# The weight sums of a 20-product down projection: from POOL to DVE

## Chip, cores and metric

The kernel runs on one core of one Trainium2 chip. The metric is the device time of one execution, in microseconds (us), as a median of several runs. Lower is better.

## What is computed

The reference is one step of a small streaming encoder with two layers, on 1024 prompt frames and 128 sample frames (8 streams of 16), 1152 tokens of width 1024 in all, float32 throughout:

```python
for layer in range(DEPTH):                       # DEPTH = 2: layer 0 is mixer A, layer 1 is mixer B
    ...                                          # norm, projections, chunked attention, output projection
    hp = hp + mlp(hp, g_mlp[layer], w_up[layer], w_down[layer])
    hs = hs + mlp(hs, g_mlp[layer], w_up[layer], w_down[layer])

def mlp(x, g_norm, w_up, w_down):
    return jnp.square(jax.nn.relu(rmsnorm(x, g_norm) @ w_up)) @ w_down
```

`w_up` is 1024 x 4096, `w_down` is 4096 x 1024. The change touches the last product of `mlp`, the down projection.

## The kernel before

Each layer runs through attention (with its projections), `wo_phase`, `mlp_up` and `mlp_down`. A float32 matmul is done in three passes: an operand is split into a high part, which ScalarE (ACT) rounds off in a cast (L128), and a low part, which VectorE (DVE) forms by subtracting the high part (L134, in `split`). Then `mm3` (L744) adds high x high, high x low and low x high into one bank of PSUM. These are the lines L746, L747 and L748 of the profile.

**The down projection** (`mlp_down`, L971) multiplies the block matrices by a scheme with 20 products instead of the usual number. It runs it twice in a layer, once for each half of the 4096 inner columns, so a layer has 40 products in a list `seq`. One product n takes:

- `a`: a combination of blocks of the activations, formed already in `mlp_up` (`forms_even`, `forms_odd`; the sums of tiles h and ht, L923 to L968) and stored by POOL's queue to DRAM (`hd`, L911). It is loaded by SP (`load_h`) and split in place: ACT casts, DVE subtracts (a<-a).
- `w`: one block of `w_down`, or a sum or difference of two. The raw blocks `r` (128 x 2048 elements, 1 MB) are loaded by SP (`load_w`). Where the product needs two of them, `add_w` (L1051) forms the sum in a buffer `s` (two of them, in turn); this is L1067. The last four products of a layer write it over a raw block instead. `split_w` (L1069) then splits w and a.
- 36 matmuls: three banks of 128 tokens each x 4 blocks of the inner dimension x 3 passes.
- additions: the three banks are added to or subtracted from tiles `x` of the residual (L1119), for none, one or two of the six output blocks.

The tables `W_FORMS`, `OUT_FORMS` and `CHAINS` at the top of the file say which blocks a product reads and which outputs it is added to. By these tables a layer has 32 products with two raw blocks and 8 with one; 8 products that add nothing, 23 that add one set of three banks, 9 that add two sets. Products of one chain go on accumulating in the same three banks, so within a chain the next product's first matmul on a bank waits for the L1119 that reads this bank. There are six banks in turn (`c=(6, 1)`), two buffers w and three a.

**Order.** A planner orders the instructions of each engine ahead of time: it simulates the program in time and gives each engine, among the instructions that are ready, the one that stands first in the program. Each engine then runs its queue strictly in that order and waits on semaphores. In the program the loop over n issues the loads for product n + 3, the splits for n + 1, the sum for n + 2, the matmuls and additions of n, and then the loads of further a. SP issues its loads in one fixed chain (`load`, L1030).

Of the kernel before, what the change touches and what calls it, by code (L numbers as in the profile page):

```python
# [11 lines left out]
ALU = mybir.AluOpType  # L12
# [82 lines left out]
class Build:  # L95
# [875 lines left out]
    def mlp_down(self, layer, out):  # L971
        nc = self.nc
        tt = nc.vector.tensor_tensor
        wd = self.ins["w_down"][layer].rearrange("(c g h p) n -> g h p c n", g=2, h=2, p=P)
        with ExitStack() as st:
# [11 lines left out]
            def take(tag):  # L987
                return slots.pop(tag) if tag in slots else fresh(tag)
# [60 lines left out]
            src = {}  # L1049

            def add_w(n):  # L1051
                if n >= total:
                    return
                s, p, g, *_, raws = seq[n]
                used = [(r, f) for r, f in enumerate(W_FORMS[p]) if f != "."]
                g = g if p not in NEG_H[s] else 1
                x, y = (raws[used[i][0]] for i in (0, -1))
                if len(used) == 1:
                    assert g == 1
                    src[n] = x  # L1060
                    return
                src[n] = x if n >= total - TAIL + 2 else take(f"s{n % 2}")
                plus = used[1][1] == "+"
                assert g == 1 or not plus
                if g < 0:
                    x, y = y, x
                nc.gpsimd.tensor_tensor(src[n], x, y, ALU.add if plus else ALU.subtract)  # L1067

            def split_w(n):  # L1069
                if n >= total:  # L1070
# [15 lines left out]
            for n in range(AHEAD):  # L1086
# [3 lines left out]
                if n in X_AT:  # L1090
                    load_x(X_AT[n])
            add_w(0)
            split_w(0)
            add_w(1)
            for n, (s, p, g, first, final, reads, _) in enumerate(seq):
                if layer == 0 and n == RANK:
# [3 lines left out]
                if n + AHEAD in X_AT:  # L1100
                    load_x(X_AT[n + AHEAD])
                split_w(n + 1)
                add_w(n + 2)
                if first:
                    banks = [self.psum("c", [P, 512], "ps_c") for _ in range(3)]
                a, w = aa.pop(n), ws.pop(n)
                for i in range(3):
# [9 lines left out]
                    for o, v in reads:  # L1117
                        x = xs[PARTS[o // 2][i]][:, N[o % 2]]
# [717 lines left out]
```

## Time and profile before

| | before |
|---|---|
| median of 3 runs | 2477.91 us (2471.18 to 2479.93) |
| the profiled execution, its own time | 2474.45 us |
| span from its first to its last instruction | 2472.3 us |
| granted TensorE clock, mean | 0.980 |
| first layer's down stage, about | 803 to 1198 us |
| second layer's down stage, about | 2079 to 2468 us |
| sums (L1067) | 64 on POOL |

In the profile PE is the matmul engine and PEld its weight loads, DVE is VectorE, ACT is ScalarE, POOL is GpSimd and SP the queue that issues most DMAs. A row of a group reads: line, engine, operation, what it writes <- what it reads, shape, count | busy us, mean ns of one | idle us of the engine just before, and what ended it. Matmuls overlap one another, so the spacing of their starts says more than their durations.

### The profile page before, as it was taken

The numbers are of one execution on the slowest core, as the hardware profiler recorded it, in microseconds if no ns is written. First come the engines' busy times: TensorE is split into PE (matmuls) and PEld (weight loads), VectorE is DVE, ScalarE is ACT, GpSimd is POOL, SyncE is SP. The second block draws the span as 40 slices with busy tenths as digits, with TensorE's granted clock in tenths as the row PEclk, the third lists the DMA queues.
The fourth block names the chain that finished last, engine by engine and source line by source line (L and its number), as shares of the span: only waits on it lengthen the run. The fifth ranks groups of instructions, "written<-read, shape, count | busy, mean of one in ns | idle before, by whom it ended". The sixth has DMA issues, their size and how long they took to land.

```text
span 2472.3 us, 33316 instructions
## 1 busy us (share of the span) xinstructions
PE 2311.3 (93%) x11429; PEld 1911.4 (77%) x11429; DVE 1848.3 (75%) x3128; ACT 1273.0 (51%) x2503; POOL 914.6 (37%) x956
## 2 busy tenths in 40 slices
PE   8998999999999789989999999998999998899989
PEld 6787877888888667767778788786888887677767
DVE  6788787665665888999577867877656566798995
ACT  3777674655555333333277766655555554233332
POOL 4434334122322554553233434344222223444650
PEclk9999999999999999999999999998999999899999
DMA  7445554243434643525544655543334336524523
GB/s 249 126 116 162 167 175 166 92 146 116 163 131 178 250 150 105 197 79 195 167 144 133 189 163 169 181 157 129 125 119 149 131 130 225 187 94 141 175 74 130
DMA packets 216376, 375.38 MB, mean 152 GB/s; under 512 B 51144, under 2 KB 125840, under 8 KB 216208
## 3 DMA queue, kind: packets, MB, share of 16 engines
q1 hardware_dynamic: 193136, 300.89, 37.8%
q0 software_dynamic: 21776, 67.65, 7.5%
q10 hardware_dynamic: 1296, 4.72, 0.5%
q8 instruction: 90, 1.47, 0.3%
q14 instruction: 78, 0.64, 0.1%
HBM read 241.23 MB, written 130.90 MB: 151 GB/s over the span
## 4 chain that ended last, share of the span: by engine, by line
PE 62%; DVE 18%; DMA 9%; issue 6%; ACT 3%; POOL 1%; SPq 0%; DVEq 0%; ACTq 0%; POOLq 0%
DVE a L134 5%; PE ps_x L746 5%; PE ps_x L748 5%; PE ps_x L747 5%; DVE w L134 3%; DMA a<-hd 3%; DVE x L1119 3%; PE ps_mm L217 3%; PE ps_c L746 3%; PE ps_c L747 3%; PE ps_c L748 3%; PE ps_mm L219 3%; PE ps_mm L218 3%; PE ps_y L748 2%; PE ps_y L747 2%
## 5 line engine op out<-in xcount | busy, mean ns | idle before, releaser
L746 PE MATMUL ps_c<-w,a 128*128 128x512 f32 x960 | 386.3, 402 | 62.2 <-DVE x L1119 54.7
L747 PE MATMUL ps_c<-w,a 128*128 128x512 f32 x960 | 385.0, 401 | 24.0 <-DVE w L134 23.9
L1067 POOL TENSOR_TENSOR s<-r,r 128x2048 f32<-128x2048 f32 x56 | 291.2, 5202 | 281.2 <-DVE w L134 160.4
L748 PE MATMUL ps_c<-w,a 128*128 128x512 f32 x960 | 383.1, 399 | 5.4 <-DVE a L134 5.4
L911 POOL DMA_DIRECT2D hd<-h x272 | 147.9, 544 | 582.4 <-ACT h L820 280.0
L134 DVE TENSOR_TENSOR a<-a 128x1536 fp32r<-128x1536 f32 x80 | 258.5, 3232 | 46.4 <-ACT a L128 46.4
L746 PEld LDWEIGHTS ps_c<-w,a 128*128 128x128 f32 x960 | 185.9, 194 | 113.7 <-DVE x L1119 36.9
L747 PEld LDWEIGHTS ps_c<-w,a 128*128 128x128 f32 x960 | 185.9, 194 | 67.6 <-DVE w L134 29.4
L128 ACT CAST a<-a 128x1536 fp32r<-128x1536 f32 x80 | 118.5, 1481 | 213.9 <-DMA a<-hd 213.8
L748 PEld LDWEIGHTS ps_c<-w,a 128*128 128x128 f32 x960 | 186.0, 194 | 47.1 <-DVE a L134 8.0
L128 ACT CAST w<-s 128x2048 fp32r<-128x2048 f32 x56 | 107.1, 1912 | 212.0 <-PE ps_c L748 177.9
L134 DVE TENSOR_TENSOR w<-s,w 128x2048 fp32r<-128x2048 f32 x56 | 176.3, 3150 | 21.8 <-ACT w L128 21.7
L1119 DVE TENSOR_TENSOR x<-x,ps_c 128x512 f32<-128x512 f32 x246 | 158.8, 676 | 35.7 <-PE ps_c L748 35.5
L217 PE MATMUL ps_mm<-w,hh 128*128 128x512 f32 x432 | 172.9, 401 | 6.5 <-POOL w L185 2.1
L219 PE MATMUL ps_mm<-w,hl 128*128 128x512 f32 x432 | 171.9, 399 | 1.2 <-DMA hl<-hTd 1.0
L218 PE MATMUL ps_mm<-w,hh 128*128 128x512 f32 x432 | 170.9, 396 | 1.4 <-DVE w L190 1.1
L746 PE MATMUL ps_x<-sx,w 128*128 128x512 f32 (+1 forms) x408 | 158.9, 390 | 3.4 <-ACT h L867 2.5
L747 PE MATMUL ps_x<-sx,w 128*128 128x512 f32 (+1 forms) x408 | 155.2, 380 | 0.0
L748 PE MATMUL ps_x<-sx,w 128*128 128x512 f32 (+1 forms) x408 | 155.2, 380 | 0.0
L128 ACT CAST w<-ru 128x512 fp32r<-128x512 f32 (+1 forms) x160 | 110.0, 708 | 84.4 <-PE ps_y L747 32.0
L134 DVE TENSOR_TENSOR ptl<-ps_tr,pth 128x512 fp32r<-128x512 f32 x180 | 122.4, 685 | 23.5 <-ACT pth L128 18.0
L134 DVE TENSOR_TENSOR w<-ru,w 128x512 fp32r<-128x512 f32 (+1 forms) x160 | 126.6, 793 | 15.2 <-ACT w L128 15.1
(280 smaller groups left out, 5972.6 us busy)
## 6 DMA issues: line engine op xcount, KB each, us to landing
a<-hd SPq DMA_DIRECT2D x80, 768.0 KB, 4.2
hd<-h POOLq DMA_DIRECT2D x272, 192.0 KB, 2.5
ru<-in_w_up SPq DMA_DIRECT2D x64, 512.0 KB, 3.8
r<-in_w_down SPq DMA_DIRECT2D x32, 1024.0 KB, 8.7
x<-xd SPq DMA_DIRECT2D x41, 512.0 KB, 6.4
o<-oTd SPq DMA_DIRECT2D x52, 256.0 KB, 4.4
xd<-xo SPq DMA_DIRECT2D x18, 512.0 KB, 2.8
xo<-xd SPq DMA_DIRECT2D x18, 512.0 KB, 3.7
```

What stands on the lines that cost most here:

```text
L128: a = nc.scalar.copy(hi, src)
L134: return a, e.tensor_tensor(lo, src, hi.bitcast(F32), ALU.subtract)
L217: nc.tensor.matmul(ps, a, w[:, 0, k, :], start=(k == 0), stop=False)
L218: nc.tensor.matmul(ps, a, w[:, 1, k, :], start=False, stop=False)
L219: self.lp = nc.tensor.matmul(ps, b, w[:, 0, k, :], start=False, stop=(k == KC - 1))
L746: a = mm(ps, ah, bh, start=first, stop=False, skip_group_check=True)
L747: mm(ps, ah, bl, start=False, stop=False, skip_group_check=True)
L748: return a, mm(ps, al, bh, start=False, stop=last, skip_group_check=True)
L911: return lambda p, z: self.nc.gpsimd.dma_start(self.hd[c // 4][:, p, c % 4], z)
L1067: nc.gpsimd.tensor_tensor(src[n], x, y, ALU.add if plus else ALU.subtract)
L1119: tt(x, x, banks[i], ALU.add if v > 0 else ALU.subtract)
```

## The change

The sums and differences of two weight blocks are formed by VectorE instead of GpSimd. `tt` is `nc.vector.tensor_tensor`, set at the top of `mlp_down`. Operands, shapes and the place in the program stay.

```diff
@@ add_w, in mlp_down @@
                 if g < 0:
                     x, y = y, x
-                nc.gpsimd.tensor_tensor(src[n], x, y, ALU.add if plus else ALU.subtract)
+                tt(src[n], x, y, ALU.add if plus else ALU.subtract)
```

## Prediction, made before the change was run

> **What bounds the kernel now.** I read the page first (busy shares, costliest groups), then the two down stages by windows, then the rows of the sums, and last the engines' rows in order of time.
>
> ```profile
> span 2472.3 us, 33316 instructions
> ...
> PE 2311.3 (93%) x11429; PEld 1911.4 (77%) x11429; DVE 1848.3 (75%) x3128; ACT 1273.0 (51%) x2503; POOL 914.6 (37%) x956
> ...
> L746 PE MATMUL ps_c<-w,a 128*128 128x512 f32 x960 | 386.3, 402 | 62.2 <-DVE x L1119 54.7
> L747 PE MATMUL ps_c<-w,a 128*128 128x512 f32 x960 | 385.0, 401 | 24.0 <-DVE w L134 23.9
> L1067 POOL TENSOR_TENSOR s<-r,r 128x2048 f32<-128x2048 f32 x56 | 291.2, 5202 | 281.2 <-DVE w L134 160.4
> ```
> ```profile
> L134 DVE TENSOR_TENSOR a<-a 128x1536 fp32r<-128x1536 f32 x80 | 258.5, 3232 | 46.4 <-ACT a L128 46.4
> L134 DVE TENSOR_TENSOR w<-s,w 128x2048 fp32r<-128x2048 f32 x56 | 176.3, 3150 | 21.8 <-ACT w L128 21.7
> ...
> L134 DVE TENSOR_TENSOR w<-r,w 128x2048 fp32r<-128x2048 f32 x24 | 68.4, 2849 | 18.3 <-ACT w L128 18.3
> ```
>
> Over the span PE looks like the bound, but where it idles in the down stage it waits for DVE: 54.7 us for L1119 (a product's banks added into x) and 23.9 us for L134 (the low half of w). The sums of the change (L1067) are POOL's, and POOL idles 281.2 us ahead of them, most of it until DVE has released a buffer s. So POOL is not the bound of the stage by its own work. The next view says how much of the stage is not matmul. It is cut into products 0 to 5, 6 to 35 and 36 to 39 of each layer (36 matmuls a product: 216, 1080, 144).
>
> ```profile
> 803.60:871.80 68.20, 53.86 (x216) 41.98 (x215) 11.84 (x18) 0.92 0.72 253
> 871.80:1157.30 285.50, 254.62 (x1080) 205.08 (x1081) 62.84 (x98) 0.98 0.40 134
> 1157.30:1197.20 39.90, 35.62 (x145) 27.66 (x143) 4.08 (x6) 0.96 0.52 181
> 2079.10:2151.10 72.00, 56.06 (x216) 44.34 (x216) 11.80 (x18) 0.86 0.58 210
> 2151.10:2433.10 282.00, 257.28 (x1081) 207.52 (x1081) 62.72 (x98) 0.96 0.36 122
> 2433.10:2468.00 34.90, 33.40 (x145) 26.69 (x143) 4.17 (x7) 1.00 0.38 127
> ```
>
> (Columns: the stretch, its length, busy time of PE, PEld and DVE on this tile, granted clock, DMA share, GB/s.) An undisturbed product takes 8.16 us: three matmuls start 0.68 us apart (the first two PE rows below), and a product has twelve such threes. So the six stretches would take 49.0, 244.8, 32.6, 49.0, 244.8 and 32.6 us; they are longer by 19.2, 40.7, 7.3, 23.0, 37.2 and 2.3 us. Together 129.7 us is all that these stages can give. Why the 30 middle products take 9.5 us each is seen in the rows by time:
>
> ```profile
> 2194.99 2.28 DVE L134 TENSOR_TENSOR w<-s,w 128x2048 fp32r<-128x2048 f32 x1
> 2197.19 0.67 DVE L1119 TENSOR_TENSOR x<-x,ps_c 128x512 f32<-128x512 f32 x1
> 2197.79 5.79 DVE L134 TENSOR_TENSOR a<-a 128x1536 fp32r<-128x1536 f32 x1
> 2203.50 1.27 DVE L1119 TENSOR_TENSOR x<-x,ps_c 128x512 f32<-128x512 f32 x2
> 2204.70 2.27 DVE L134 TENSOR_TENSOR w<-s,w 128x2048 fp32r<-128x2048 f32 x1
> 2206.90 1.74 DVE L134 TENSOR_TENSOR a<-a 128x1536 fp32r<-128x1536 f32 x1
> ```
> ```profile
> 2197.34 4.62 POOL L1067 TENSOR_TENSOR s<-r,r 128x2048 f32<-128x2048 f32 x1 [5.09 <-DVE w L134]
> 2207.05 6.07 POOL L1067 TENSOR_TENSOR s<-r,r 128x2048 f32<-128x2048 f32 x1 [5.09 <-DVE w L134]
> ```
> ```profile
> 2201.90 0.39 PE L748 MATMUL ps_c<-w,a 128*128 128x512 f32 x1
> ...
> 2202.58 0.39 PE L748 MATMUL ps_c<-w,a 128*128 128x512 f32 x1
> 2204.23 0.50 PE L746 MATMUL ps_c<-w,a 128*128 128x512 f32 x1 [1.26 <-DVE x L1119]
> ```
>
> (Columns: start, duration, engine, instruction.) The same a<-a subtraction takes 5.79 us when a POOL sum began shortly before it, and 1.74 us when it began first; then the sum takes 6.07 instead of 4.62 us. The first sum ends at 2201.96 and a<-a at 2203.58, that is 1.62 us later: it did nothing until POOL had finished. The two engines exclude each other here, and whichever starts second waits. DVE is thereby busy without a break: w, x, a, x, x, and again w 9.71 us after the last (2194.99 to 2204.70), while PE waits 1.26 us for an x addition that stands behind a<-a. DVE's lost time sets the pace.
>
> **The change, part by part.** The rows for the prices:
>
> ```profile
>   DMA r<-in_w_down: 116.7, 15
> ```
> ```profile
> L134 DVE TENSOR_TENSOR a<-a x80: 1739/1759/6099, 795.5 to 2457.4; 128x1536 fp32r<-128x1536 f32 x80
> ```
>
> (The first row: how long POOL sat idle ahead of L1067 until r had landed, and how often. The second: minimum, median and maximum of a<-a in ns.) Added on DVE: 64 sums, 56 into s by the row above and 8 in place by the code (the last four of a layer). DVE has no plain sum of this shape in the trace; the nearest row is w<-s,w, the same two SBUF operands of 2048 elements, at 2.28 us where nothing holds it (2194.99 above). From below it could not be under a<-a's 1.74 us (1536 elements), from above 3.15 us, the mean of w<-s,w with its waits. I take 2.28, since the waits were for POOL: 64 x 2.28 = 146 us.
>
> Removed from DVE: the waits inside its own instructions. a<-a falls from 3.23 to 1.76 us, 80 x 1.47 = 118 us; w<-s,w from 3.15 to 2.28 us, 56 x 0.87 = 49 us. The 24 w split straight from r fall from 2.85 to 2.28 us, 14 us. In the first products two small sums of the stage before are held too:
>
> ```profile
> L943 DVE TENSOR_TENSOR ht<-h 128x384 f32<-128x384 f32 x1 | 5.0, 4974 | 0.0
> L939 DVE TENSOR_TENSOR ht<-h 128x384 f32<-128x384 f32 x1 | 4.9, 4879 | 0.0
> ...
> L935 DVE TENSOR_TENSOR h<-h 128x384 f32<-128x384 f32 x1 | 0.5, 547 | 0.0
> ```
>
> Those two (groups of the stretch from 780 to 860 us) lose 4.4 and 4.3 us against the 0.55 of the third. I take it that the second layer has such a pair as well: 17 us. In all 118 + 49 + 14 + 17 = 198 us leave and 146 come: DVE is relieved by about 52 us while it takes over all the sums. POOL is empty in these stages afterwards but for the stores of h. At the start of a stage these queue behind the sums; they come out earlier at no cost. The sums' sources are loaded as before by SP, whose queue holds the loads of a and x too; nothing is moved on it. Outside the two stages the instructions are the same; the planner may place some of them otherwise, which I set at nothing, since no row says which way.
>
> What is on the path: the middle products. A product with one bank set to add costs DVE 2.28 (w) + 1.74 (a) + 2.28 (sum) + 1.94 (three x: 0.67 and 1.27) = 8.24 us, and consecutive instructions overlap by a little (the 9.71 us cycle holds 10.01 us of them), so about 7.9 us against PE's 8.16. PE takes over as the bound, narrowly. The scheme's tables give 23 such products of 40 in a layer; 8 add nothing (6.0 us) and 9 add two bank sets (9.7 us). Eight products need no sum (2.28 us less). Following both through the order, only five stretches of a product ask DVE for 9.7 us: 5 x 1.5 = 8 us, and 2 us for order: 10 us left of 40.7, 10 of 37.2. The sum is off PE's path as long as w waits for the release of its buffer, not for s: ACT's cast of w starts when PE ends the product two before, and then that cast and the 2.28 us of w fill only half of a product.
>
> Start: PE waits there for loads and for x, of which the held pair explains 8.7 us less the two new sums, 4.6 us. I take 5 us off each: 14 and 18 left. End: no sum stands in those products; the 7.3 and 2.3 us stay. Left over: 14 + 10 + 7 + 18 + 10 + 2 = 61 of 129.7, so 69 us are saved. The profiled execution took 2474.45 us (span 2472.3), so it would take 2405; the median of the three runs, 2477.91, lies 3.5 us above it, and against the median that is 2409 us.
>
> Part of this comes through the clock, so it hangs on long idle times going away:
>
> ```profile
> 2174.54 0.79 PE L746 MATMUL ps_c<-w,a 128*128 128x512 f32 x1 [3.69 <-DVE x L1119]
> ...
> 2179.82 0.42 PE L746 MATMUL ps_c<-w,a 128*128 128x512 f32 x1
> ```
>
> After an idle time of 3.69 us the next twelve matmuls take 5.28 us (from row to row, eleven lie between) instead of 12 x 0.227 = 2.72: a tail of 2.6 us beyond the gap itself.
>
> **The rivals.** *Slower: sums that block DVE.* DVE runs its queue in order. POOL waited 116.7 us, 15 times, for r to arrive, with little else behind it. If the planner puts a sum into DVE's queue ahead of its landing, the splits and the x additions behind it wait as well, and PE after them. For it: 7.8 us a wait is more than the 4 us or so by which w is early. Against it: several of these waits lie at the start, where PE waits for loads of the same queue, and a sum two products ahead can be planned late. It decides from 69 / 15 = 4.6 us of each wait that reaches PE. With 5.5 us of each and ten slow-clock tails: 2409 + 83 + 26 = 2518 us.
>
> *Slower: a saturated DVE.* The middle stretches have DVE busy nearly throughout; if its busy time were work, 32 x 2.28 = 73 us a stage would lengthen both:
>
> ```profile
> 803.00:1198.00 395.00, 345.50 (x1453) 276.31 (x1452) 341.85 (x239) 136.53 (x89) 183.99 (x60) 0.97 0.47 160
> 2079.00:2468.00 389.00, 346.86 (x1442) 278.63 (x1440) 335.94 (x217) 132.63 (x82) 173.69 (x46) 0.95 0.40 139
> ```
>
> DVE (third figure) would stand at 415 and 409 us in stages of 395 and 389: 20 us longer each, 2478 + 40 = 2518 us. The 1.74 beside 5.79 us speaks against it. The Trainium skill, Perfetto Trace Analysis, section "Optimizing Scalar/DVE Operations", advises moving work off a saturated DVE, to GPSIMD even, which is the other way from this change; it adds that the two share an SBUF read port so that such a move might not help, and the trace agrees with this second half (a<-a held to 5.79 us behind a sum).
>
> *No change.* A sum on DVE comes just before an x addition for which PE waits. If half of the 64 do, 32 x 2.28 = 73 us come back: 2409 + 73 = 2482 us. The rows leave room for a sum behind w, where PE has just got its bank, so I hold it unlikely.
>
> **How the numbers follow.** Forecast 0.74; blocked sums 0.13, saturated DVE 0.05, no change 0.08. The forecast's own range is 2380 (all 78 us of the middle and 20 of the starts saved) to 2440 (half of the middle kept). Within 0.5%, about what a measurement of this kernel can tell from no change, means 2465.5 to 2490.3 us. The no-change case reaches out of it at both ends, 0.02 of it to the faster side. Faster 0.76, same 0.06, slower 0.18. For 8 in 10 the range goes to 2495, which leaves out the larger part of the slower cases, and begins at 2380.
>
> **What would show it.** Right: L1067 on DVE at about 2.3 us; a<-a at a mean near 1.8 and w<-s,w near 2.3 us; PE's idle time for L1119 well under 54.7 us; the middle stretches near 255 us, at a clock of 0.99 or 1.00; DVE's busy time some 50 us lower. Wrong: DVE idle before L1067 for r<-in_w_down with PE waiting behind it (first rival); L1067 or a<-a above 3 us with POOL empty, which would refute the exclusion; PE's waits for L1119 as long as before while a<-a is short (no change).

## The result and the profile after

With the sums on DVE the kernel takes 2402.07 us (median of 4 runs, 2399.86 to 2404.34). The kernel before, beside it, took 2474.55 us. The ratio is 0.9708, with a 95% interval of 0.968 to 0.9736: about 72 us less. The profiled execution has a span of 2399.8 us, 72.5 us less than before.

The page of the kernel after (busy shares, then the groups that answer to those shown of before; columns as there):

```profile
PE 2291.6 (95%) x11429; PEld 1903.1 (79%) x11429; DVE 1787.2 (74%) x3192; ACT 1272.6 (53%) x2503; POOL 573.2 (24%) x892
...
L746 PE MATMUL ps_c<-w,a 128*128 128x512 f32 x960 | 380.3, 396 | 29.7 <-ACT a L128 15.9
L747 PE MATMUL ps_c<-w,a 128*128 128x512 f32 x960 | 378.9, 395 | 5.2 <-DVE w L134 5.2
...
L134 DVE TENSOR_TENSOR a<-a 128x1536 fp32r<-128x1536 f32 x80 | 140.4, 1755 | 56.0 <-ACT a L128 56.0
...
L134 DVE TENSOR_TENSOR w<-s,w 128x2048 fp32r<-128x2048 f32 x56 | 127.9, 2284 | 15.5 <-ACT w L128 15.5
...
L1067 DVE TENSOR_TENSOR s<-r,r 128x2048 f32<-128x2048 f32 x56 | 127.7, 2284 | 2.8 <-DMA r<-in_w_down 2.8
```

DVE has 64 instructions more and is 61 us less busy, because a<-a went from 3232 to 1755 ns and w<-s,w from 3150 to 2284 ns. PE's idle time before L746 fell from 62.2 to 29.7 us, and the largest part of it is no longer DVE's x addition (54.7 us before, 13.7 now) but ACT, which waits for a load of a. The wait for w at L747 fell from 23.9 to 5.2 us.

The down stages of the kernel after, cut into products 0 to 5, 6 to 35 and 36 to 39 of each layer (stretch, length, busy PE, PEld and DVE on the banks, granted clock, DMA share, GB/s):

```profile
805.30:871.30 66.00, 54.93 (x217) 43.72 (x217) 11.82 (x18) 0.90 0.68 245
871.30:1127.20 255.90, 247.57 (x1081) 201.85 (x1080) 63.90 (x98) 1.00 0.46 153
1127.20:1167.60 40.40, 36.86 (x145) 28.46 (x143) 4.13 (x7) 0.92 0.53 181
2045.10:2110.10 65.00, 53.84 (x216) 42.64 (x216) 11.81 (x18) 0.92 0.64 234
2110.10:2360.80 250.70, 246.47 (x1082) 202.16 (x1081) 63.84 (x98) 1.00 0.41 138
2360.80:2395.50 34.70, 33.32 (x145) 26.64 (x143) 4.26 (x8) 1.00 0.39 128
```

The two middle stretches lost 29.6 and 31.3 us (285.5 and 282.0 before), the starts 2.2 and 7.0, the ends nothing. Sum of the six: 782.5 us before, 712.7 after, so 69.8 of the 72.5 us lie where the sums are. The clock in the middle is 1.00, where it was 0.98 and 0.96.

The steady cycle, DVE's rows by time in the kernel after (start, duration):

```profile
944.93 2.29 DVE L134 TENSOR_TENSOR w<-s,w 128x2048 fp32r<-128x2048 f32 x1 [0.16 <-ACT w L128]
947.14 0.68 DVE L1119 TENSOR_TENSOR x<-x,ps_c 128x512 f32<-128x512 f32 x1
947.74 2.28 DVE L1067 TENSOR_TENSOR s<-r,r 128x2048 f32<-128x2048 f32 x1
949.94 1.75 DVE L134 TENSOR_TENSOR a<-a 128x1536 fp32r<-128x1536 f32 x1
951.61 1.28 DVE L1119 TENSOR_TENSOR x<-x,ps_c 128x512 f32<-128x512 f32 x2
953.13 2.29 DVE L134 TENSOR_TENSOR w<-s,w 128x2048 fp32r<-128x2048 f32 x1 [0.25 <-ACT w L128]
```

Five pieces of work, w to w in 8.20 us, and 0.16 to 0.25 us of slack ahead of each w: DVE now waits, by way of ACT's cast, for PE. Before, the same cycle without the sum took 9.71 us.

### The profile page after: what moved, and what is told of

Read it like the earlier page. It is cut to its first block, busy times and chain, and to the rows that moved or that the text cites. A ratio compares the mean times of both kernels' runs of the same rounds, so it can differ in the third digit from the quotient of the medians.

```text
span 2399.8 us, 33255 instructions
## 1 busy us (share of the span) xinstructions
PE 2291.6 (95%) x11429; PEld 1903.1 (79%) x11429; DVE 1787.2 (74%) x3192; ACT 1272.6 (53%) x2503; POOL 573.2 (24%) x892
## 4 chain that ended last, share of the span: by engine, by line
PE 68%; DVE 14%; DMA 8%; issue 4%; ACT 3%; POOL 1%; SPq 1%; ACTq 0%; DVEq 0%; POOLq 0%
PE ps_x L746 5%; PE ps_x L748 5%; PE ps_x L747 5%; PE ps_c L748 5%; PE ps_c L746 5%; PE ps_c L747 5%; PE ps_mm L219 4%; PE ps_mm L217 4%; PE ps_mm L218 4%; PE ps_y L748 2%; PE ps_y L747 2%; PE ps_y L746 2%; DVE w L134 2%; PE ps_tr L324 2%; DVE x L1119 2%
## 5 line engine op out<-in xcount | busy, mean ns | idle before, releaser
L746 PE MATMUL ps_c<-w,a 128*128 128x512 f32 x960 | 380.3, 396 | 29.7 <-ACT a L128 15.9
L747 PE MATMUL ps_c<-w,a 128*128 128x512 f32 x960 | 378.9, 395 | 5.2 <-DVE w L134 5.2
L748 PE MATMUL ps_c<-w,a 128*128 128x512 f32 x960 | 378.8, 395 | 4.7 <-DVE a L134 4.5
L128 ACT CAST a<-a 128x1536 fp32r<-128x1536 f32 x80 | 118.6, 1482 | 242.5 <-DMA a<-hd 240.1
L746 PEld LDWEIGHTS ps_c<-w,a 128*128 128x128 f32 x960 | 183.0, 191 | 75.5 <-ACT a L128 18.0
L748 PEld LDWEIGHTS ps_c<-w,a 128*128 128x128 f32 x960 | 182.8, 190 | 46.9 <-DVE a L134 8.5
L747 PEld LDWEIGHTS ps_c<-w,a 128*128 128x128 f32 x960 | 182.9, 191 | 44.0 <-DVE w L134 6.6
L134 DVE TENSOR_TENSOR a<-a 128x1536 fp32r<-128x1536 f32 x80 | 140.4, 1755 | 56.0 <-ACT a L128 56.0
L128 ACT CAST w<-s 128x2048 fp32r<-128x2048 f32 x56 | 107.2, 1914 | 126.7 <-PE ps_c L748 119.0
L746 PE MATMUL ps_x<-sx,w 128*128 128x512 f32 (+1 forms) x408 | 158.4, 388 | 3.7 <-ACT h L867 2.7
L747 PE MATMUL ps_x<-sx,w 128*128 128x512 f32 (+1 forms) x408 | 154.8, 379 | 0.0
L128 ACT CAST w<-ru 128x512 fp32r<-128x512 f32 (+1 forms) x160 | 110.0, 708 | 84.4 <-PE ps_y L747 32.0
L134 DVE TENSOR_TENSOR w<-s,w 128x2048 fp32r<-128x2048 f32 x56 | 127.9, 2284 | 15.5 <-ACT w L128 15.5
L1067 DVE TENSOR_TENSOR s<-r,r 128x2048 f32<-128x2048 f32 x56 | 127.7, 2284 | 2.8 <-DMA r<-in_w_down 2.8
```

Of the source, the lines that this page charges most:

```text
L128: a = nc.scalar.copy(hi, src)
L134: return a, e.tensor_tensor(lo, src, hi.bitcast(F32), ALU.subtract)
L746: a = mm(ps, ah, bh, start=first, stop=False, skip_group_check=True)
L747: mm(ps, ah, bl, start=False, stop=False, skip_group_check=True)
L748: return a, mm(ps, al, bh, start=False, stop=last, skip_group_check=True)
L1067: tt(src[n], x, y, ALU.add if plus else ALU.subtract)
```

## Experiments

The theory to be tested is the prediction's: POOL's sums and DVE's instructions with two operands in SBUF shut each other out, and the time that DVE stood still set PE's pace. Rivals: the sums are simply ready sooner on DVE (2.28 us instead of 4.6 or more; ACT waited 34.1 us for POOL's sums); or the planner rearranged the program. On the last, the traces of the two kernels have the same order of instructions on PE and on ACT throughout both down stages, and DVE's differs by a few places beside the inserted sums.

**POOL kept busy, with work that nobody needs.** Behind each sum on DVE, POOL reads one column of s (so that it starts at that point) and then works on a scratch tile in place (`gap`, which the kernel before holds but doesn't use). These kernels differ in the kind and the number of POOL's instructions only. The first, with two operands (the line that names `gap` is left out):

```diff
+            tt_junk = self.gap[:, 0:512]
+            nc.gpsimd.memset(tt_junk, 0.0)
...
+                nc.gpsimd.tensor_copy(tt_junk[:, 0:1], src[n][:, 0, 0:1])
+                for _ in range(4):
+                    nc.gpsimd.tensor_tensor(tt_junk, tt_junk, tt_junk, ALU.subtract)
```

> The changed kernel, and behind each of the 64 sums on DVE four idle POOL subtractions of 128x512 (about 1.28 us each by L700 to L703, 5.1 us together), on a scratch tile that nobody reads. Exclusion theory (DVE and POOL instructions with two SBUF operands shut each other out): per product with a sum 5.1 us of POOL and 6.3 us of DVE (w, a, sum) can't overlap, 11.4 us against PE's 8.16, so a<-a and w<-s,w above 2.3 and 2.8 us in the mean and a time of 2480 to 2610 us. Lateness theory (the gain came from sums that are ready sooner than POOL's were): a<-a stays at 1.76 us and the time at 2395 to 2412 us.

Measured: 2468.07 us, ratio to before 0.9973 (0.9959 to 0.9986). Its groups of the scratch work and of DVE:

```profile
L1073 POOL TENSOR_TENSOR gap<-gap 128x512 f32<-128x512 f32 x256 | 521.9, 2039 | 19.6
L134 DVE TENSOR_TENSOR a<-a 128x1536 fp32r<-128x1536 f32 x80 | 173.3, 2166 | 39.9 <-ACT a L128 39.9
L134 DVE TENSOR_TENSOR w<-s,w 128x2048 fp32r<-128x2048 f32 x56 | 146.9, 2624 | 7.5 <-ACT w L128 7.5
```

The sums stand where they do in the kernel after, and 66 of the 72 us are gone; by windows, some 51 us of this lie in the middle stretches (280.8 and 277.2 us). By itself this doesn't settle the lateness: the sums are held too. ACT's casts of w, the first to need a sum, waited for them as follows, before, after and here (behind the bar: idle time, and what ended it):

```profile
L128 ACT CAST w<-s 128x2048 fp32r<-128x2048 f32 x56 | 107.1, 1912 | 212.0 <-PE ps_c L748 177.9 <-POOL s L1067 34.1
L128 ACT CAST w<-s 128x2048 fp32r<-128x2048 f32 x56 | 107.2, 1914 | 126.7 <-PE ps_c L748 119.0 <-DVE s L1067 5.2 <-DVE a L134 2.6
L128 ACT CAST w<-s 128x2048 fp32r<-128x2048 f32 x56 | 107.0, 1911 | 184.8 <-PE ps_c L748 155.0 <-DVE s L1070 24.3 <-DVE x L1125 5.5
```

The kernel with the sums in pieces, below, decides that. Here the time is 12 us below the expected range, a<-a at 2.17, not above 2.3 us, and w<-s,w at 2.62, not above 2.8: DVE is held less than a sum of both engines' work would have it, and POOL more (a subtraction that takes 1.04 us at the least takes 2.04 in the mean). What DVE loses here is 33 us in a<-a (80 x 0.41), 19 us in w<-s,w and some 29 us in the other w and the sums.

**No operand read.** The same with eight memsets in place of the loop's four subtractions.

```diff
-                for _ in range(4):
-                    nc.gpsimd.tensor_tensor(tt_junk, tt_junk, tt_junk, ALU.subtract)
+                for _ in range(8):
+                    nc.gpsimd.memset(tt_junk, 0.0)
```

> As pool_two, but eight POOL memsets of 128x512 (no operand read, only written; about 0.5 us each from L583's 0.21 us for 128x128). The Trainium skill, SBUF — State Buffer, section "SBUF: two separate sides", says that a DVE instruction with two SBUF inputs is shut out only by a GpSimd one that reads SBUF. By that rule a<-a stays at 1.76 us and the time at 2395 to 2412 us. If writing alone shuts out as well, a<-a above 2.1 us and 2440 to 2560 us. This kernel also shows whether the added small read of s by POOL costs anything by itself.

Measured: 2401.26 us, ratio 0.9712 (0.9696 to 0.9728), the time of the kernel after.

```profile
L1073 POOL MEMSET gap<- 128x512 f32 x512 | 270.4, 528 | 28.9
L134 DVE TENSOR_TENSOR a<-a 128x1536 fp32r<-128x1536 f32 x80 | 140.3, 1753 | 53.7 <-ACT a L128 53.6
```

512 memsets, 270 us of POOL, and a<-a is untouched. A busy POOL costs nothing; what it reads does. The Trainium skill (SBUF — State Buffer, "SBUF: two separate sides") states that a DVE instruction with two SBUF inputs is shut out only by a GpSimd instruction that reads SBUF. The traces agree: beside subtractions, which read, a<-a took 2.17 us, beside memsets 1.75. On the DVE side too it is the operands that matter: x<-x,ps_c, whose second operand is in PSUM, has a maximum of 689 ns over its 246 instances in the kernel before, in pool_two and in pool_one alike. Two operands are not the whole condition, though: L1141, an instruction that reads one small tile (16x256) and one column of it, took 4.10 us beside a POOL sum in the kernel before and 0.34 in the kernel after. The small read of s costs nothing by itself either.

**One operand read.** Seven multiplications by 1.0 in place of the four subtractions, later four.

```diff
-                for _ in range(4):
-                    nc.gpsimd.tensor_tensor(tt_junk, tt_junk, tt_junk, ALU.subtract)
+                for _ in range(7):
+                    nc.gpsimd.tensor_scalar(tt_junk, tt_junk, 1.0, 1.0, ALU.mult, ALU.mult)
```

> As pool_two, but seven POOL multiplications of 128x512 by a constant (one SBUF operand, about 0.72 us each by L526) instead of the four subtractions. If any POOL instruction that reads SBUF shuts DVE's two-operand instructions out, a<-a rises above 2.2 us and the time to 2460 to 2600 us; if it takes two operands on both sides, 2395 to 2412 us with a<-a at 1.76 us. Lateness theory: 2395 to 2412 us.

Measured: 2494.85 us, ratio 1.0085 (1.0065 to 1.0105), slower than the kernel before, but not for the reason expected:

```profile
L1073 POOL TENSOR_SCALAR gap<-gap 128x512 f32<-128x512 f32 x448 | 626.1, 1397 | 36.4
L134 DVE TENSOR_TENSOR a<-a 128x1536 fp32r<-128x1536 f32 x80 | 151.7, 1896 | 55.4 <-ACT a L128 55.4
...
L1070 DVE TENSOR_TENSOR s<-r,r 128x2048 f32<-128x2048 f32 x56 | 129.8, 2321 | 64.8 <-POOL gap L1071 64.0 <-POOL gap L1073 0.7
```

a<-a rose only to 1.90 us. It was POOL that stood still: a multiplication takes 0.63 us unheld, 1.40 in the mean. It fell behind, and the next sum on DVE then waited 64 us for POOL's read of s. The time is inside the expected range by another mechanism, so it settles nothing; hence fewer of them:

```diff
-                for _ in range(7):
+                for _ in range(4):
```

> As pool_one, with four multiplications of 128x512 in place of seven. In pool_one they were themselves held (1.40 us in the mean, 0.63 at best), fell behind the products, and the sums on DVE then waited 64 us for POOL's read of s; a<-a rose only to 1.90 us. With four, POOL has 4 x 1.4 + 0.7 = 6.3 us a product and keeps up with PE's 8.16. If a POOL instruction with one SBUF operand shuts DVE out as well, only for as long as each lasts: a<-a 1.82 to 2.0 us, no wait for s, 2405 to 2430 us. If pool_one's loss was the wait for s alone: a<-a 1.76 us, 2395 to 2405 us.

Measured: 2429.23 us, ratio 0.9831 (0.9802 to 0.986).

```profile
L1073 POOL TENSOR_SCALAR gap<-gap 128x512 f32<-128x512 f32 x256 | 380.9, 1488 | 21.1
L134 DVE TENSOR_TENSOR a<-a 128x1536 fp32r<-128x1536 f32 x80 | 148.7, 1858 | 59.8 <-ACT a L128 59.8
...
L1070 DVE TENSOR_TENSOR s<-r,r 128x2048 f32<-128x2048 f32 x56 | 130.4, 2332 | 5.2 <-DMA r<-in_w_down 5.0
```

The wait for s is gone and a<-a is at 1.86 us: a POOL instruction with one operand shuts DVE out as well, for a short time (a<-a takes 2.17 us at most). The 27 us that it costs against the kernel after are more than DVE's own loss, about 18 us (8 in a<-a, 7 in w<-s,w, 3 in s). PE's idle time for a (ACT a L128) grew from 15.9 to 25.6 us; the scratch work stands in POOL's queue among the stores of h that the start of the stage waits for, and by windows the two starts are 4 and 6 us longer. But the middle stretches, in which POOL stores nothing, are longer too, by 14 and 6 us (270.2 and 256.9), and there PE's largest waits are for DVE's x additions (13.4 and 6.5 us, against 6.3 and 3.8 in the kernel after). So DVE's path has the larger part; an exact division isn't to be had, since the profiled execution (2438.55 us) is 9 us above the median.

**The same sums on POOL, in four pieces.** This leaves all work where it was before.

```diff
-                nc.gpsimd.tensor_tensor(src[n], x, y, ALU.add if plus else ALU.subtract)
+                for j in range(4):
+                    nc.gpsimd.tensor_tensor(
+                        src[n][:, j], x[:, j], y[:, j], ALU.add if plus else ALU.subtract
+                    )
```

> The kernel before, each of POOL's 64 sums cut into four of 128x512. If a DVE instruction is held by the one POOL instruction that runs when it starts, and no longer, a<-a has at most 1.74 + 1.28 = 3.0 us (2.60 in pool_two) instead of 5.8, its mean falls to about 2.2 us, and with no sum on DVE the middle products come near PE's pace: 2400 to 2445 us. If DVE is held for the whole run of POOL's instructions, a<-a keeps its 3.2 us and the time stays at 2468 to 2485 us. What could spoil the first: POOL is then the one that waits between its pieces (2.04 us a piece in pool_two, 8.2 us a sum), and w comes late for its sum.

Measured: 2422.52 us, ratio 0.9804 (0.9773 to 0.9834).

```profile
L1068 POOL TENSOR_TENSOR s<-r,r 128x512 f32<-128x512 f32 x224 | 462.0, 2099 | 82.0 <-DMA r<-in_w_down 62.7 <-DVE w L134 17.4 <-PE ps_x L748 1.8
```

```profile
L134 DVE TENSOR_TENSOR a<-a x80: 1740/2133/2917, 795.9 to 2405.1; 128x1536 fp32r<-128x1536 f32 x80
```

```profile
L128 ACT CAST w<-s 128x2048 fp32r<-128x2048 f32 x56 | 107.0, 1911 | 231.4 <-POOL s L1068 154.3 <-DVE x L1122 50.2 <-PE ps_c L748 26.9
```

Two thirds of the gain come from cutting the instruction. a<-a now takes 2.92 us at most (6.10 before; minimum, median, maximum in ns), below the expected 3.0: a DVE instruction is held by the one POOL instruction that is running, and gets in before the next. The price goes to POOL, where a piece takes 2.10 instead of 1.28 us, 8.4 us a sum, and the sums come later than before: ACT's casts of w waited 154.3 us for them, where it had been 34.1. The sums are later and the kernel is faster, so lateness is not what the change removed. The last third may be this lateness, or what DVE still loses (a<-a at 2.16 us in the mean, against 1.76 after); the two were not separated.

**One layer alone.**

```diff
-                tt(src[n], x, y, ALU.add if plus else ALU.subtract)
+                (tt if layer == 0 else nc.gpsimd.tensor_tensor)(
+                    src[n], x, y, ALU.add if plus else ALU.subtract
+                )
```

> Only the first layer's 32 sums on DVE, the second layer's on POOL as before. If the gain is local to each down stage (exclusion, PE's stalls), the first stage is as in the changed kernel (362 us instead of 394) and the second as before (389): about 2474 - 32 - 2 = 2440 us, 2430 to 2448. If the gain came from a rearranged plan elsewhere, it needn't be split that way: 2402 or 2474 us.

Measured: 2441.38 us, ratio 0.986 (0.9831 to 0.9888). Its two down stages, cut by windows on the banks:

```profile
805.40:1168.00 362.60, 339.74 (x1440) 273.89 (x1439) 79.95 (x122) 0.97 0.51 173
2050.60:2438.00 387.40, 343.52 (x1440) 275.45 (x1439) 78.59 (x122) 0.96 0.40 139
```

The first is as in the kernel after (362), the second as before (389). So the gain is made in each stage by itself.

**No sums.** This kernel leaves the sums out: w is split from one of its two raw blocks, and both are still loaded.

```diff
-                src[n] = x if n >= total - TAIL + 2 else take(f"s{n % 2}")
...
-                tt(src[n], x, y, ALU.add if plus else ALU.subtract)
+                src[n] = x
```

> The changed kernel with the 64 sums left out: w is split from the first of the two raw blocks. Exclusion theory with PE as the bound after the change: the sums' 146 us on DVE are nearly all covered, so only the stalls at products with two bank sets go: 2375 to 2400 us. If DVE still were the bound of the down stages, a third or more of the 146 us would come off: below 2350 us. What the sums cost in all on POOL is then the kernel before less this one.

Measured: 2375.82 us, ratio 0.9611 (0.9593 to 0.9629). Of the 146 us of sums on DVE some 26 reach the end of the kernel; PE covers the rest. On POOL the same sums cost 98 us (2474.14 less 2375.82), though ACT had waited only 34.1 us for their results.

**The start of the stage**, where the forecast was least good. SP loads the x tiles of part 0 ahead of the next a and r, and stands at this load for 30.4 us, until a store of ht to `hd` has landed. In the kernel after:

```profile
801.97 31.84 SPq L1031 DMA_DIRECT2D x<-xd  x3
834.21 0.32 SPq L1031 DMA_DIRECT2D a<-hd  x1
834.59 0.53 SPq L1031 DMA_DIRECT2D r<-in_w_down  x1
```

and PE's first matmul of product 3, which needs that a:

```profile
842.55 0.79 PE L746 MATMUL ps_c<-w,a 128*128 128x512 f32 x1 [7.09 <-ACT a L128]
```

The edit has the load issued with the blocks of product 6 instead of product 3:

```diff
-X_AT = {0: 2, 1: 1, 3: 0}
+X_AT = {0: 2, 1: 1, 6: 0}
```

Three kernels: this edit on the kernel after, the kernel after once more beside it, and this edit on the kernel before.

> The changed kernel with the load of the x tiles of part 0 (tokens 5, 6, 7) issued with product 6's blocks instead of product 3's; product 8 is the first to use them. The start of each stage is the part where the prediction was off (5 us forecast off the first start, 2 measured). Theory: SP's queue stands for 33.7 us at this load until the last store of h has landed, with a of product 3 and r of product 4 behind it, and PE waits for that a (7.1 and 5.9 us) after running slow; the load moved back, both stages lose 10 to 15 us: 2372 to 2390 us. Rival: a of product 3 or r of product 4 waits for the same stores by its own buffer, or the stores' DMA traffic sets the pace: 2395 to 2410 us.

> The changed kernel itself, for a comparison on this chip: 2395 to 2410 us.

> The kernel before (sums on POOL), with the load of the x tiles of part 0 issued as late as in xlate. If the start's wait for that load is independent of who forms the sums, it gains what xlate gains on the changed kernel, about 20 us: 2450 to 2460 us. If POOL's sums hold the first products anyway, less than 8 us: 2466 to 2476 us.

Measured: 2379.20 us (ratio 0.9612, 0.9587 to 0.9637), 2399.35 us (0.9694, 0.9673 to 0.9716) and 2457.72 us (0.994, 0.9923 to 0.9957). The starts of xlate by windows:

```profile
801.90:857.30 55.40, 51.28 (x216) 41.50 (x216) 11.70 (x18) 0.97 0.87 302
2036.10:2090.60 54.50, 51.06 (x216) 41.59 (x216) 11.78 (x18) 0.97 0.79 278
```

They are shorter by 10.6 and 10.5 us than in the kernel after (66.0 and 65.0): the theory held, and the load order was a second limit. On the kernel before the edit brings 16 us, a little less than the 20 beside it. With both, the kernel is 96 us faster than before, the fastest version here with all the sums in it.

## Why the prediction was right, point by point

Forecast 2409 us, measured 2402.07; in differences, 69 us against 72. About 3.4 of the 7 us between the two times come from the base: the forecast was counted from 2477.91 us, and the kernel before took 2474.55 beside the kernel after.

- **Prices.** The sum on DVE was taken from w<-s,w at 2.28 us; it takes 2.284. a<-a at 1.76: 1.755. w<-s,w and w<-r,w at 2.28: 2.284 and 2.288. DVE's relief was put at 52 us and is 61. Some 4 us of the difference are L1141, which I had not priced; added up one by one, DVE's instructions are 55 us shorter, and the other 6 us are more overlap between instructions in a row.
- **Who sets the pace.** PE took over with 8.20 us a cycle, where 7.9 us of DVE's work against 8.16 had been worked out.
- **Middle products.** 10 and 10 us were to be left over the undisturbed 244.8; it is 11.1 and 5.9. From the first matmul of a product to that of the next, few products exceed 8.16 us: 30 and 33 in both layers (by 2.4 and about 1.5 us), each of which follows a product with two sets of additions, as forecast, and in the first layer 7 and 8 too (3.4 and 2.0), behind such products as well. So four stretches of the first layer and two of the second were short of DVE time, where five in each had been forecast. At product 30 there is also something of the no-change rival's kind: an in-place sum stands ahead of the additions for which PE waits.

```profile
1073.90 2.28 DVE L1067 TENSOR_TENSOR r<-r,r 128x2048 f32<-128x2048 f32 x1
1076.10 1.75 DVE L134 TENSOR_TENSOR a<-a 128x1536 fp32r<-128x1536 f32 x1
1077.77 2.47 DVE L1119 TENSOR_TENSOR x<-x,ps_c 128x512 f32<-128x512 f32 x4
```
```profile
1079.10 0.50 PE L746 MATMUL ps_c<-w,a 128*128 128x512 f32 x1 [2.00 <-DVE x L1119]
```

- **Starts.** The weakest term: 14 and 18 us were to be left, and 17.0 and 16.0 are (66.0 and 65.0 less 49.0). That the two errors, 3 us one way and 2 the other, nearly cancel in the total is luck. The freed DVE time did help the x additions there (product 2 waits 1.2 us for them, 5.6 before), but then PE waits 7.09 us for a of product 3, which stands in SP's queue behind the x load. I had named loads as a reason and still taken 5 us off both starts alike; the kernel with the later x load shows what held them.
- **Ends.** 7 and 2 us were to stay: 7.8 and 2.1.
- **Blocked sums.** DVE waited 2.8 us for r ahead of L1067, 3 times, where POOL had waited 116.7 us, 15 times. Nearly all sums stand in DVE's queue where r has landed already. The rival's condition didn't arise.
- **Saturated DVE.** Some 200 of the 678 us that DVE was busy in the two stages were standing still: busy time in the trace includes the time for which an instruction is shut out (the 5.79 us of an a<-a that takes 1.74).

## What to carry to other kernels

Compare an instruction's minimum with its mean before calling its engine saturated: a<-a had 1.74 against 3.23 us, and the difference was another engine's work. Where DVE and POOL both run instructions that read two large SBUF operands, POOL's share can be paid for twice, once by itself and once by DVE; moving it to DVE can relieve DVE. If it must stay on POOL, cut it into pieces: here DVE was held for one POOL instruction at a time only. POOL's results then come later.

## What was not expected of the hardware

The exclusion is uneven. In these runs DVE waits at most for the rest of one POOL instruction (a<-a's maximum: 6.10 us beside sums of 4.6 us, 2.92 beside pieces of 1.28 us), while POOL is held longer. With several short instructions in a row it takes in the mean 2.10 us for a piece of 1.28, 2.04 for a subtraction of 1.04 and 1.49 for a multiplication of 0.63; and in the kernel before, one sum of 4.6 us took 11.99 (from 857.83 us): DVE ran a<-a, w<-s,w and a<-a in that time, none of them held, and the sum ended 4.5 us after the last. Durations on POOL are rough in this profile. A POOL memset of 128x512 (0.53 us) does not take part in it at all, and a POOL multiplication with one SBUF operand does.
